# Softmax weights kept in PSUM, their sums split between GpSimd and the value matmul, and the first recurrence unit prepared inside the attention

## The chip, the cores and the metric

The kernel runs on one core of one Trainium2 chip. The metric is the device time of one execution in microseconds (us). The core has five engines that run their own instruction queues and meet through semaphores: TensorE (PE: matmul, with its weight loads as PEld), VectorE (DVE), ScalarE (ACT), GpSimd (POOL) and SyncE (SP, which issues DMAs here). Each engine works through its queue in order: an instruction that waits holds up everything behind it on that engine.

## The reference

One layer of a hybrid backbone runs on 1024 latent and 256 context tokens of width 1024. What matters here is the token mixer. Both branches read the same projected input `z = h @ w_in`:

```python
s = jnp.einsum('bqkgd,bskd->bkgqs', qi, kf) * scale
p = jax.nn.softmax(s, axis=-1)
return jnp.einsum('bkgqs,bskd->bqkgd', p, vf)
...
kv = jnp.einsum('bhnck,bhncv->bhnkv', k_end, v)
def step(s, inp):
    dec, kv_n = inp
    return dec[..., None] * s + kv_n, s
```

The attention has 8 query heads of 64 and 2 key heads; latent queries see 512 cached and 1024 latent keys, context queries the 256 context keys. The second branch is a gated linear recurrence with 4 heads, run forwards and backwards. Gates, an output projection and a squared-ReLU MLP follow.

## The kernel before

Every product of weights and activations that matters is made with values split into a high part (fp32r, the format that PE takes at full pace) and a low part, value minus high part; three matmuls stand for one. After a front part (normalisation, queries, keys and values, up to about 177 us) the attention runs, then the recurrence, then the projections and the MLP.

**The attention** (`attention`, class `Unit`) has 20 units: for each of the two key heads, eight units of 512 latent queries of one head against 12 blocks of 128 keys, and two units that hold 256 context queries of two heads against 2 blocks. A unit does this:

- `load_q`, `load_q2` load the queries (SP); `top` multiplies queries and keys (high parts) block by block and VectorE takes the maximum of each row; `top_row` transposes the four columns of maxima into rows, which four small DMAs put into row 64 of the second query operand, so that the score matmul subtracts the maximum by itself.
- `score(k)` for each key block: two matmuls (L725) into a bank of the PSUM ring `s`; ACT takes the exponential (L727) and a copy rounded to fp32r, the high part (L729); VectorE makes the low part (L730); POOL adds the exponentials into the accumulator `pacc` (L735, L737).
- `value`: two blocks at a time, each with two matmuls (L748) of the high and the low weights against V. V's 128 columns are V's 64 high columns and its 64 low ones, so rows 0 to 63 and 64 to 127 of the bank `ps_v` are added at the end (L752, L753).
- `sums`, `scale`: four fp32 matmuls of one column (L759) sum `pacc` over the keys, VectorE takes the reciprocal, PE transposes it, ACT copies it, POOL stores it to DRAM (`RR`), loads it back over 64 rows and multiplies (L773); SP stores the result.

**What sets the order.** PE's order is written out by hand. `attention` makes a list of events with a time in slots, one slot being one key block, sorts it and issues it. Between events a `Filler` hands out matmuls of the projections for the recurrence (L318 to L320 and L335 to L337, 277 us of them). Other engines' queues and SP's are ordered by a scheduler at build time. The recurrence (`hgrn`, class `HUnit`) has 24 units; `prep` loads a gate and a query block (`uf`, `uq`), makes two running products on VectorE (L891, L892) and several products on POOL and VectorE; `keys_t` transposes the keys on PE (L953). Before, the first `prep` stands in `hgrn`, after the attention and its filler have ended.

**Where the data lie.** SBUF tiles come from rings named by letters, with as many buffers as `RINGS` says; a new tile waits for the release of an old one. PSUM has eight banks of 128 rows by 512 fp32 columns, in the rings g, v, s and t.

Of the kernel before, what the change touches and what calls it, by code (L numbers as in the profile page):

```python
# [45 lines left out]
def build(ctx, tc, I, O, C):  # L46
# [25 lines left out]

    PSB = {"g": 2, "v": 1, "s": 3, "t": 2}
    ring_of_two, turn = [True], [0]

    def PS(tag, shape=(P, 512)):
        if tag == "g" and not ring_of_two:
            turn[0] += 1
            tag = "v" if turn[0] % 3 == 0 else tag
        return ps.tile(list(shape), F32, tag=tag, name="ps_" + tag, bufs=PSB[tag])  # L80

# [26 lines left out]
    def store(out, in_):  # L108
        g_.dma_start(out=f32(out), in_=f32(in_))  # L109

    def f32(ap):
        return ap.bitcast(F32)
# [486 lines left out]
    for idx in range(len(steps)):  # L599
# [23 lines left out]
        if kc == 0:  # L623
            if t > 0:
                front_prep(evs)
            banks = [PS(x) for x in ("sssv", "ggss", "sv")[t]]
        cols_next = t == 0 and kc % 2 == 1 and kc < KC - 1
# [43 lines left out]
    class Unit:  # L671
# [49 lines left out]
        def score(self, k):  # L721
            kg, b = self.kt[k]
            pq = PS("s")
            for var, q in enumerate((self.q1, self.q2)):
                pe.matmul(pq, K[self.g][var][kg][:, b * P:(b + 1) * P], q, start=(var == 0), stop=(var == 1))  # L725
            e = S(name="pexp")
            s_.activation(e, pq, AF.Exp)  # L727
            hi, lo = S(dt=F32R, name="pTh"), S(dt=F32R, name="pTl%d" % (k % 2))
            s_.activation(hi, e, AF.Copy)  # L729
            v.tensor_tensor(lo, e, f32(hi), op=ALU.subtract)  # L730
            if k == 0:
                self.acc = e
            elif k == 1:
                first, self.acc = self.acc, S(name="pacc")
                g_.tensor_tensor(self.acc, first, e, op=ALU.add)  # L735
            else:
                g_.tensor_tensor(self.acc, self.acc, e, op=ALU.add)  # L737
            self.pt[k] = hi, lo

        def value(self, p2):  # L740

            if p2 == 0:
                self.pv = PS("v")
            last = self.nb - 1
            for k in (2 * p2, 2 * p2 + 1):
                kg, b = self.kt[k]
                for j, x in enumerate(self.pt.pop(k)):
                    pe.matmul(self.pv, V[self.g][kg][:, b, :], x, start=(k == 0 and j == 0), stop=(k == last and j == 1))  # L748
            if k == last:
                tm, self.o = S((64, 512), name="pvt"), S((64, 512), name="oa")  # L750
                with tc.high_priority(offset=400):
                    s_.activation(tm, self.pv[64:128], AF.Copy)  # L752
                    v.tensor_tensor(self.o, self.pv[0:64], tm, op=ALU.add)  # L753

        def sums(self):

            pt = PS("t")
            for b in range(4):
                pe.matmul(pt[:, b:b + 1], self.acc[:, b * P:(b + 1) * P], one0[:, 0:1], start=True, stop=True)  # L759
            self.rs = T(4, "rs")  # L760
            v.reciprocal(self.rs, pt[:, 0:4])

        def scale(self):

            pt = PS("t")
            pe.transpose(pt[0:4, 0:P], self.rs, ident)
            r = S((4, P), name="prow")
            s_.activation(r, pt[0:4, 0:P], AF.Copy)
            row = RR[self.h][self.t]
            store(row.rearrange("o (b n) -> (o b) n", b=4), r)  # L770
            o, rb = self.o, S((64, 512), name="prb")
            g_.dma_start(out=rb, in_=row.broadcast_to([64, 512]))
            g_.tensor_tensor(o, o, rb, op=ALU.mult)  # L773
            oa = OA[self.h // 2][self.t]
            if self.t < 2:
                d0 = (self.h % 2) * 64
                dma(oa[d0:d0 + 64, :], o)
            else:
                dma(oa.rearrange("(h d) n -> d h n", h=2), self.view(o))

    RR = [[DR((1, 512), "RR%d_%d" % (h, t)) for t in range(3)] for h in range(8)]
    K = [[[None] * 4 for _ in range(2)] for _ in range(2)]
    V = [[None] * 4 for _ in range(2)]

    def load_k(g, kg, var):
# [8 lines left out]
    def load_v(g, kg):  # L794
        V[g][kg] = S((P, KG[kg] // P, P), F32R, name="Vl")
        dma(V[g][kg], VS[kg][:, :, g, :])

    def attention(fill):
        units = []
# [6 lines left out]
        for u in units:  # L806
            ev = []
            if u.t == 2:
                ev += [(-13.3, load_k, (u.g, 3, 0)), (-3.3, load_v, (u.g, 3))]
            elif u.g not in seen:  # L810
                seen.add(u.g)
                ev += [(a, load_k, (u.g, kg, 0)) for kg, a in enumerate((-13.4, -13.3, -13.2))]
# [12 lines left out]
        for a, f, x in events:  # L825
            fill.to((a - e0) / (e1 - e0))
            f(*x)
        ring_of_two.pop()

# [43 lines left out]
    class HUnit:  # L873
# [8 lines left out]
        def prep(self):  # L882
# [5 lines left out]

            c, e = S(name="ucp"), S(name="usf")
            if d == 0:  # L890
# [139 lines left out]
    def hgrn(fill):  # L1030

        units = [HUnit(h, d, t) for h in range(4) for d, t in ((0, 0), (0, 1), (1, 1), (1, 0), (0, 2), (1, 2))]
        fwd = {u.h: {} for u in units}
# [6 lines left out]
        tot, done, st = sum(share), 0.0, None  # L1040
        units[0].prep()
        units[0].keys_t()
# [60 lines left out]
    while pending:  # L1103
        fz.add(1.0)
        flush(1.0)
    attention(fz)
    fz.rest()
    R = S(name="R")
    g_.memset(R, 0.0)
    g_.memset(R.rearrange("p (c i) -> p c i", i=32)[:, :, 0:1], 1.0)  # L1110
    fg = Filler(with_ada([z_ch(GL + 256 * c, gl_consume(c)) for c in range(8)], 10), 194.0)
# [693 lines left out]
```

## Time and profile before

| | us |
|---|---|
| median of three runs | 2119.05 (2113.95 to 2119.84) |
| profiled execution | 2115.53 |
| its span | 2113.4 |
| PE busy | 2015.6 |
| VectorE, ScalarE, GpSimd busy | 1437.2, 958.2, 675.8 |

The profile lists busy time by engine, groups of instructions by source line, waits (who waited for whom, total, number, longest), and a timeline. A row names line, engine, operation, output<-inputs and size. PE's records overlap: one of 512 columns is shown with 0.39 us, while the next one starts 0.23 us after it. A wait is put down to the instruction whose signal came last.

### The profile page before, as it was taken

To read this page: it belongs to the slowest core of one execution; us is meant where nothing else is said; L and a number is where in the kernel's file an instruction comes from. 1 tells how busy PE (TensorE), PEld (TensorE's weight loads), DVE (VectorE), ACT (ScalarE), POOL (GpSimd) and SP (SyncE) were. 2 spreads that over 40 slices of the span, in tenths; PEclk is the share of its full clock that TensorE was granted. 3 is DMA by queue.
4 is the path that set the end of the run, shared out by engine and by line. 5 is a ranking of instruction groups with operands and counts; after the bars stand their busy time and mean duration, and the time that the engine had idled before them with its cause. 6 is when DMAs were issued, how large, how long until landed. Compare 5 with 4: busy or idle time off the path is not lost.

```text
span 2113.4 us, 31691 instructions
## 1 busy us (share of the span) xinstructions
PE 2015.6 (95%) x11436; PEld 1696.6 (80%) x11436; DVE 1437.2 (68%) x2385; ACT 958.2 (45%) x1802; POOL 675.8 (32%) x715
## 2 busy tenths in 40 slices
PE   6899999999999959999999999999999999999998
PEld 4687788877778848888888888998888888888886
DVE  4784777787787776797543734876666666567786
ACT  4763565555555512222330323765545444333442
POOL 1471455665454754554302200222122210000010
PEclk9999999999999979999999999999999999999999
DMA  9464222142221244554554532674444469545773
GB/s 293 129 189 145 89 91 91 51 145 71 80 78 58 78 135 123 177 173 152 159 172 140 185 111 109 215 224 161 148 160 147 168 223 372 181 147 178 219 261 127
DMA packets 236957, 325.21 MB, mean 154 GB/s; under 512 B 22024, under 2 KB 153264, under 8 KB 236800
## 3 DMA queue, kind: packets, MB, share of 16 engines
q1 hardware_dynamic: 222784, 280.87, 41.6%
q0 software_dynamic: 14016, 42.32, 5.7%
q8 instruction: 90, 1.47, 0.3%
q14 instruction: 67, 0.55, 0.1%
HBM read 235.46 MB, written 87.61 MB: 153 GB/s over the span
## 4 chain that ended last, share of the span: by engine, by line
PE 42%; issue 15%; POOL 4%; DVE 3%; DMA 2%; ACT 1%; SPq 0%; POOLq 0%; DVEq 0%; ACTq 0%
POOL AF L109 4%; PE ps_g L318 3%; PE ps_g L319 3%; PE ps_g L320 3%; PE ps_s L1606 2%; PE ps_s L1607 2%; PE ps_s L1608 2%; PE ps_v L318 1%; PE ps_g L1608 1%; PE ps_t L1606 1%; PE ps_g L1606 1%; PE ps_g L1607 1%; PE ps_t L1607 1%; PE ps_t L1608 1%; PE ps_v L320 1%
## 5 line engine op out<-in xcount | busy, mean ns | idle before, releaser
L737 POOL TENSOR_TENSOR pacc<-pacc,pexp 128x512 f32<-128x512 f32 x160 | 230.2, 1439 | 111.7 <-ACT pexp L727 68.6
L730 DVE TENSOR_TENSOR pTl<-pexp,pTh 128x512 fp32r<-128x512 f32 x200 | 229.8, 1152 | 48.7 <-ACT pTh L729 47.3
L318 PE MATMUL ps_g<-hs,wsp 128*128 128x512 f32 (+1 forms) x688 | 249.9, 363 | 0.0
L320 PE MATMUL ps_g<-hs,wsp 128*128 128x512 f32 (+1 forms) x688 | 241.6, 351 | 0.8 <-DVE wsp L290 0.8
L319 PE MATMUL ps_g<-hs,wsp 128*128 128x512 f32 (+1 forms) x688 | 241.8, 351 | 0.0
L289 ACT ACTIVATE wsp<-wraw 128x1024 fp32r<-128x1024 f32 x110 | 109.4, 996 | 267.9 <-PE ps_g L319 70.4
L290 DVE TENSOR_TENSOR wsp<-wraw,wsp 128x1024 fp32r<-128x1024 f32 x110 | 139.2, 1266 | 130.4 <-ACT wsp L289 130.1
L727 ACT ACTIVATE pexp<-ps_s 128x512 f32<-128x512 f32 x200 | 119.3, 597 | 163.9 <-PE ps_s L725 124.7
L708 DVE TENSOR_REDUCE mx<-ps_t 128x1 f32<-128x512 f32 (+1 forms) x208 | 136.8, 664 | 72.5 <-PE ps_t L707 71.7
L289 ACT ACTIVATE ah<-ar 128x640 fp32r<-128x640 f32 (+1 forms) x112 | 81.0, 724 | 189.3 <-PE ps_v L1607 102.3
L318 PEld LDWEIGHTS ps_g<-hs,wsp 128*128 128x128 f32 x688 | 131.4, 191 | 20.3 <-issue 2.9
L320 PEld LDWEIGHTS ps_g<-hs,wsp 128*128 128x128 f32 x688 | 131.0, 190 | 18.9 <-DVE wsp L290 1.0
L290 DVE TENSOR_TENSOR ah<-ar,ah 128x640 fp32r<-128x640 f32 (+1 forms) x112 | 89.8, 802 | 80.4 <-ACT ah L289 79.2
L319 PEld LDWEIGHTS ps_g<-hs,wsp 128*128 128x128 f32 x688 | 131.3, 191 | 16.5
L729 ACT ACTIVATE pTh<-pexp 128x512 fp32r<-128x512 f32 x200 | 126.0, 630 | 7.6
L171 POOL TENSOR_TENSOR frst<-ms,mexp 128x1 f32<-128x1 f32 x10 | 11.1, 1111 | 363.3 <-DVE ssf L1695 278.5
L335 PE MATMUL ps_g<-wsp,hs 128*128 128x256 f32 x400 | 115.8, 289 | 0.0
L337 PE MATMUL ps_g<-wsp,hs 128*128 128x256 f32 x400 | 112.8, 282 | 0.0
L336 PE MATMUL ps_g<-wsp,hs 128*128 128x256 f32 x400 | 112.7, 282 | 0.0
L707 PE MATMUL ps_t<-Kl,Ql 128*128 128x512 f32 x192 | 78.6, 410 | 12.5 <-DMA Ql<-QS 5.7
L725 PE MATMUL ps_s<-Q,Kl 128*128 128x512 f32 x200 | 79.0, 395 | 5.8 <-DMA Q<-mrow 3.0
L336 PEld LDWEIGHTS ps_g<-wsp,hs 128*128 128x128 f32 x400 | 75.9, 190 | 6.6
(490 smaller groups left out, 5827.3 us busy)
## 6 DMA issues: line engine op xcount, KB each, us to landing
ar<-AF SPq DMA_DIRECT2D x112, 320.0 KB, 3.3
wraw<-in_w_ff SPq DMA_DIRECT2D x32, 1024.0 KB, 5.9
wr<-in_w_ff SPq DMA_DIRECT2D x128, 256.0 KB, 4.3
wraw<-in_w_in SPq DMA_DIRECT2D x18, 1024.0 KB, 5.9
wraw<-in_w_ada SPq DMA_DIRECT2D x16, 1024.0 KB, 5.5
AF<-a POOLq DMA_DIRECT2D x48, 256.0 KB, 2.8
AF<-t POOLq DMA_DIRECT2D x48, 256.0 KB, 2.5
wa<-in_w_ada SPq DMA_DIRECT2D x32, 256.0 KB, 6.2
```

Source lines behind the costliest of these rows:

```text
L289: s_.activation(hi, raw, AF.Copy)
L290: v.tensor_tensor(lo, raw, f32(hi), op=ALU.subtract)
L318: pe.matmul(out, hi[:, k, :], mh, start=(first and k == 0), stop=False)
L319: pe.matmul(out, hi[:, k, :], ml, start=False, stop=False)
L320: pe.matmul(out, lo[:, k, :], mh, start=False, stop=(last and k == kcs - 1))
L335: pe.matmul(po[:, bb, :], mh[:, off:off + P], wh[:, k % 4, :], start=(k == 0), stop=False)
L336: pe.matmul(po[:, bb, :], mh[:, off:off + P], wl[:, k % 4, :], start=False, stop=False)
L708: v.tensor_reduce(self.mx[:, i:i + 1], pq[:, 0:n], axis=AX.X, op=ALU.max)
L727: s_.activation(e, pq, AF.Exp)
L729: s_.activation(hi, e, AF.Copy)
L730: v.tensor_tensor(lo, e, f32(hi), op=ALU.subtract)
L737: g_.tensor_tensor(self.acc, self.acc, e, op=ALU.add)
```

## The change

1. **Exponentials in PSUM.** ACT writes the exponential back into the score's bank; the high part is copied from there, and VectorE's subtraction reads the bank and the high part. A score bank is thus held until the low part is made. The ring `s` has two banks instead of three, and a new ring `w` has one.
2. **Sums in two parts.** POOL adds the high parts. The low parts go through a second value operand `V2`, V's 64 high columns beside 64 columns of ones, into the bank `ps_w`: rows 0 to 63 are low weights times V's high columns, rows 64 to 127 the sum of the low parts. (The product of low weights and V's low columns, which was made before, is left out.) One fp32 matmul with a selector (`sel1`: 64 columns of zeros, 64 of ones) adds the sum of `pacc` to rows 64 to 127. ACT copies one row, VectorE adds rows 0 to 63 to the output.
3. **The reciprocal goes through DRAM.** The row is stored (`SR`), loaded back as 128 x 4, inverted, stored (`RR`) and loaded over 64 rows: four DMAs on POOL's queue where there were two. The transpose and the four matmuls go.
4. **Order.** Loads, maxima and the row of maxima move ahead by up to 2.1 slots; a value step is now one block, issued 2.6 to 4.2 slots after its score. The query tiles move to the ring of 20 buffers, `pacc` to one of two, the low parts to one of three.
5. **First recurrence unit.** `R` and the first unit's `prep` become an event 3.8 slots before the last unit's end; `keys_t` of that unit stays at the start of `hgrn`.
6. Outside the attention every third tile of `s` comes from `w`, as one of `g` came from `v` before.

The core of the diff:

```diff
-            e = S(name="pexp")
-            s_.activation(e, pq, AF.Exp)
-            hi, lo = S(dt=F32R, name="pTh"), S(dt=F32R, name="pTl%d" % (k % 2))
-            s_.activation(hi, e, AF.Copy)
-            v.tensor_tensor(lo, e, f32(hi), op=ALU.subtract)
+            s_.activation(pq, pq, AF.Exp)
+            hi, lo = S(dt=F32R, name="pTh"), S(dt=F32R, name="pTl")
+            s_.activation(hi, pq, AF.Copy)
+            v.tensor_tensor(lo, pq, f32(hi), op=ALU.subtract)
+            if k == 1:
+                self.acc = S(name="pacc")
+            if k > 0:
+                g_.tensor_tensor(self.acc, f32(self.pt[0][0]) if k == 1 else self.acc, f32(hi), op=ALU.add)
...
+            pe.matmul(self.pv, V[self.g][kg][:, b, :], hi, start=(k == 0), stop=(k == last))
+            pe.matmul(self.pl, V2[self.g][kg][:, b, :], lo, start=(k == 0), stop=False, skip_group_check=True)
...
-            pt = PS("t")
-            for b in range(4):
-                pe.matmul(pt[:, b:b + 1], self.acc[:, b * P:(b + 1) * P], one0[:, 0:1], start=True, stop=True)
-            self.rs = T(4, "rs")
-            v.reciprocal(self.rs, pt[:, 0:4])
+            pe.matmul(self.pl, sel1[0], self.acc, start=False, stop=True, skip_group_check=True)
+            r = S(name="prow")
+            with tc.high_priority(offset=400):
+                s_.activation(r[64:65], self.pl[64:65], AF.Copy)
+                v.tensor_tensor(self.o, self.pl[0:64], self.o, op=ALU.add)
+            row, inv, rs = SR[self.h][self.t], RR[self.h][self.t], T(4, "rs")
+            store(row, r[64:65])
+            g_.dma_start(out=rs, in_=row.rearrange("o (p j) -> (o p) j", j=4))
+            v.reciprocal(rs, rs)
+            store(inv.rearrange("o (p j) -> (o p) j", j=4), rs)
...
-            ev += [(-12.9, u.load_q, ()), (-5.9, u.load_q2, ()), (-2.9, u.top_row, ())]
+            ev += [(-15.0, u.load_q, ()), (-6.9, u.load_q2, ()), (-3.4, u.top_row, ())]
-            ev += [(-11.6 + 8.2 * j / len(tops), u.top, x) for j, x in enumerate(tops)]
+            ev += [(-13.1 + 8.8 * j / len(tops), u.top, x) for j, x in enumerate(tops)]
-            ev += [(2 * p2 + 3.6, u.value, (p2,)) for p2 in range(u.nb // 2)]
-            ev += [(u.nb + 3.3, u.sums, ()), (u.nb + 4.3, u.scale, ())]
+            ev += [(k + 2.6 + max(0, 1.6 - 0.4 * k), u.value, (k,)) for k in range(u.nb)]
+            ev += [(max(u.nb + 2.2, u.nb - 1 + 4.3), u.sums, ()), (u.nb + 6, u.scale, ())]
...
+        events.append((s0 - 3.8, meanwhile, ()))
```

On PE, around a unit's sums (the sixth unit's), before: the sums write a bank of the ring t, and the next unit's first value matmuls follow four rows later. Names are those of the tiles: `ps_t`, `ps_v` banks, `pTh` and `pTl` the high and low weights.

```order
L759 MATMUL ps_t<-one_127,pacc 128x1 x4
L335 MATMUL ps_g<-wsp,hs 128x256
L336 MATMUL ps_g<-wsp,hs 128x256
L337 MATMUL ps_g<-wsp,hs 128x256
L748 MATMUL ps_v<-pTh,Vl 128x512
L748 MATMUL ps_v<-pTl_4262,Vl 128x512
L748 MATMUL ps_v<-pTh,Vl 128x512
L748 MATMUL ps_v<-pTl_4296,Vl 128x512
```

The same place now:

```order
L755 MATMUL ps_w<-pacc,sel_2303 128x512
L708 MATMUL ps_t<-Kl,Qp 128x256
L336 MATMUL ps_g<-wsp,hs 128x256
L337 MATMUL ps_g<-wsp,hs 128x256
L338 MATMUL ps_g<-wsp,hs 128x256
...
L708 MATMUL ps_t<-Kl,Ql 128x512
L726 MATMUL ps_s<-Ql,Kl 128x512
L726 MATMUL ps_s<-Q_4054,Kl 128x512
...
L745 MATMUL ps_v<-pTh,Vl 128x512
L746 MATMUL ps_w<-pTl,V_2504 128x512
```

The sums and the next unit's first low value matmul now write the same bank, `ps_w`, with filler, maxima and a score between them.

On POOL, at the last unit's end, before (`pacc` is that unit's accumulator, `ze` a gate product, `RR3_1` its reciprocal's row):

```order
L737 TENSOR_TENSOR pacc_8054<-pacc_8054,pexp_8237 128x512
L737 TENSOR_TENSOR pacc_8054<-pacc_8054,pexp_8265 128x512
L737 TENSOR_TENSOR pacc_8054<-pacc_8054,pexp_8288 128x512
L737 TENSOR_TENSOR pacc_8054<-pacc_8054,pexp_8310 128x512
L868 TENSOR_TENSOR ze_8339<-ze_8339,hnb_110 128x512
L109 DMA RR3_1_1951<-prow_8401 4x128
```

The same place now (`uf`, `usf`, `uw` are the first recurrence unit's tiles):

```order
L913 TENSOR_SCALAR uf_8055<-uf_8055 128x512
L941 TENSOR_TENSOR usf_8060<-uf_8055,usf_8060 128x512
L937 TENSOR_TENSOR uw_8080<-uq_8056,um_8065 128x512
L937 TENSOR_TENSOR uw_8082<-uq_8056,um_8065 128x512
L881 TENSOR_TENSOR ze_8121<-ze_8121,hnb_110 128x512
L937 TENSOR_TENSOR uf_8055<-usf_8060,um_8065 128x512
L735 TENSOR_TENSOR pacc_7873<-pacc_7873,pTh_8105 128x512
...
L735 TENSOR_TENSOR pacc_7873<-pacc_7873,pTh_8134 128x512
L735 TENSOR_TENSOR pacc_7873<-pacc_7873,pTh_8154 128x512
L881 TENSOR_TENSOR ze_8205<-ze_8205,hnb_110 128x512
L110 DMA SR3_1_1951<-prow_8224 16x1x32
```

Five operations of the first recurrence unit stand ahead of the last three additions, which the sums' matmul on PE needs.

On SP, the loads of the second recurrence unit (`uf`, `uq` from `FD0_0_1`, `QD0_1`), before and now:

```order
L106 DMA GD1_2_2012<-ze_8417 128x512
L106 DMA OA1_1_1921<-oa_8359 64x512
L106 DMA uv_8467<-VD0_0_2001 128x4x128
L106 DMA uf_8480<-FD0_0_1_1978 128x512
L106 DMA uq_8481<-QD0_1_1966 128x512
```

```order
L107 DMA GD1_2_2036<-ze_8272 128x512
L107 DMA uf_8297<-FD0_0_1_2002 128x512
L107 DMA uq_8298<-QD0_1_1990 128x512
L107 DMA GT0_0_2037<-ze_8394 128x512
L107 DMA OA1_1_1921<-oa_8196 64x512
```

The load stands behind the last gate store in both; it is now ahead of the last attention output's store instead of behind it.

More of the change, by code (lines that the diff above doesn't have):

```diff
@@ L70, in build @@
     sl = pool("sl")
-    PSB = {"g": 2, "v": 1, "s": 3, "t": 2}
-    ring_of_two, turn = [True], [0]
+    PSB = {"g": 2, "v": 1, "s": 2, "w": 1, "t": 2}
+    third, rings_of_two = {"g": "v", "s": "w"}, [True]
+    turn = {"g": 0, "s": 0}
     def PS(tag, shape=(P, 512)):
-        if tag == "g" and not ring_of_two:
-            turn[0] += 1
-            tag = "v" if turn[0] % 3 == 0 else tag
+        if tag in turn and not rings_of_two:
+            turn[tag] += 1
+            tag = third[tag] if turn[tag] % 3 == 0 else tag
         return ps.tile(list(shape), F32, tag=tag, name="ps_" + tag, bufs=PSB[tag])
@@ L625, in build @@
                 front_prep(evs)
-            banks = [PS(x) for x in ("sssv", "ggss", "sv")[t]]
+            banks = [PS(x) for x in ("sswv", "ggss", "wv")[t]]
         cols_next = t == 0 and kc % 2 == 1 and kc < KC - 1
@@ L725, in score, with value @@
                 pe.matmul(pq, K[self.g][var][kg][:, b * P:(b + 1) * P], q, start=(var == 0), stop=(var == 1))
-            e = S(name="pexp")
-            s_.activation(e, pq, AF.Exp)
-            hi, lo = S(dt=F32R, name="pTh"), S(dt=F32R, name="pTl%d" % (k % 2))
-            s_.activation(hi, e, AF.Copy)
-            v.tensor_tensor(lo, e, f32(hi), op=ALU.subtract)
-            if k == 0:
[L732 to L743, printed above, removed]
+            s_.activation(pq, pq, AF.Exp)
[6 more added lines that the diff above has]
+                g_.tensor_tensor(self.acc, f32(self.pt[0][0]) if k == 1 else self.acc, f32(hi), op=ALU.add)
+            self.pt[k] = hi, lo
+        def value(self, k):
+            if k == 0:
+                self.pv, self.pl = PS("v"), PS("w")
             last = self.nb - 1
[L745 to L748, printed above, removed]
+            kg, b = self.kt[k]
+            hi, lo = self.pt.pop(k)
+            pe.matmul(self.pv, V[self.g][kg][:, b, :], hi, start=(k == 0), stop=(k == last))
+            pe.matmul(self.pl, V2[self.g][kg][:, b, :], lo, start=(k == 0), stop=False, skip_group_check=True)
             if k == last:
@@ L783, in build @@
     V = [[None] * 4 for _ in range(2)]
+    V2 = [[None] * 4 for _ in range(2)]
+    sel1 = []
     def load_k(g, kg, var):
@@ L887, in prep @@
             dma(q[:, 0:n], QD[h][t])
-            c, e = S(name="ucp"), S(name="usf")
+            c, e, R = S(name="ucp"), S(name="usf"), Rs[0]
             if d == 0:
@@ L1030, in hgrn @@
     def hgrn(fill):
-        units = [HUnit(h, d, t) for h in range(4) for d, t in ((0, 0), (0, 1), (1, 1), (1, 0), (0, 2), (1, 2))]
+        units = hunits
         fwd = {u.h: {} for u in units}
@@ L1040, in hgrn @@
         tot, done, st = sum(share), 0.0, None
-        units[0].prep()
         units[0].keys_t()
```

37 lines of the change are left out of this document (23 added, 14 removed), and 4 rows, old and new, of the table RING_OF.

## The prediction

> **What bounds the kernel now.** I read the page's first part, then the busy time by windows, then the waits of PE inside the stretch that the change touches, then the timeline around its end.
>
> ```profile
> span 2113.4 us, 31691 instructions
> PE 2015.6 (95%) x11436; PEld 1696.6 (80%) x11436; DVE 1437.2 (68%) x2385; ACT 958.2 (45%) x1802; POOL 675.8 (32%) x715
> ...
> 177.00:745.00 568.00, 537.26 (x3088) 451.23 (x3087) 422.89 (x580) 318.60 (x575) 314.45 (x246) 0.99 0.27 84
> 745.00:773.00 28.00, 3.79 (x32) 2.85 (x31) 18.13 (x28) 3.37 (x6) 12.87 (x15) 0.60 0.52 169
> ```
>
> The columns of the two window rows are length, then busy time of PE, PEld, DVE, ACT and POOL, then granted clock. TensorE bounds the kernel. In the attention, from 177 to 745, it is idle 568 - 537.3 = 30.7 us of 200 key steps (2.84 us a step, called a slot below). Behind it, from 745 to 773, it is idle 24.2 us. Only these 55 us, and PE's own work, can become less.
>
> ```profile
> PE ps_t L707 <- DMA Qp<-QS: 6.1, 4, 2.8
> PE ps_t L707 <- DMA Ql<-QS: 5.7, 4, 3.5
> PE ps_t L707 <- DVE mx L708: 5.0, 8, 1.6
> PE ps_t L715 <- DVE ngm L710: 4.2, 6, 1.2
> PE ps_s L725 <- DMA Q<-mrow: 3.0, 4, 1.3
> PE ps_s L725 <- DMA Ql<-QS: 2.8, 1, 2.8
> ...
> 742.36 0.95 PE L759 MATMUL ps_t<-one,pacc 128*128 128x1 f32 x8
> 743.17 0.36 PE L335 MATMUL ps_g<-wsp,hs 128*128 128x256 f32 x1
> ...
> 745.95 1.07 PE L186 MATMUL ps_g<-wraw,ada_l 128*32 128x256 f32 x16
> 771.23 1.09 PE L953 MATMUL ps_t<-ident,usf 128*128 128x128 f32 x4 [24.21 <-DVE usf L924]
> ...
> 784.69 0.60 PE L953 MATMUL ps_t<-ident,usf 128*128 128x128 f32 x4
> ```
>
> The waits (total, times, longest) fall into 17.6 us for queries and maxima that come late by DMA, and 9.2 us for VectorE's maxima. The 24 us are the transposes of the first recurrence unit's keys waiting for a preparation that starts after the attention.
>
> **Attention: VectorE.** The 200 subtractions now read one operand from PSUM.
>
> ```profile
> L730 DVE TENSOR_TENSOR pTl<-pexp,pTh x200: 658/1150/4115, 200.1 to 736.6; 128x512 fp32r<-128x512 f32 x100
> L753 DVE TENSOR_TENSOR oa<-ps_v,pvt 64x512 f32<-64x512 f32 x20 | 13.5, 676 | 1.9 <-ACT pvt L752 1.4 <-issue 0.5
> L737 POOL TENSOR_TENSOR pacc<-pacc,pexp 128x512 f32<-128x512 f32 x160 | 230.2, 1439 | 111.7 <-ACT pexp L727 68.6 <-ACT prow L768 30.0 <-ACT mrow L717 9.0
> ```
>
> Today, with both operands in SBUF, one takes between 0.66 and 4.1 us, median 1.15. The same operation with one operand in PSUM, L753, averages 0.676 beside the same busy POOL. So VectorE loses about 200 x (1.150 - 0.676) = 95 us of its 423; the bounds are that gain and nothing. It is worth only what PE waits for VectorE's maxima, 9.2 us: I take 6 off.
>
> [...] The rows show 0.676 against an undisturbed 0.658.
>
> **Attention: loads and maxima ahead.** The query load leads its first maximum by 1.9 slots instead of 1.3 (1.7 us more), the row of maxima its first score by 3.4 instead of 2.9 (1.4 us more), and the query's ring grows from 2 to 20 buffers. Taking 1.7 us off each wait leaves 1.8 of Ql, 1.1 of Qp and 1.1 of the late score: 13.6 us go. But the loads stay in SP's queue behind output stores that now wait for two more DMA trips. I take 11 off (bounds 5 and 17.6).
>
> **Attention: the sums on PE.** Eight records and one transpose go, one fp32 matmul of 512 columns comes.
>
> ```profile
> 238.38 0.40 PE L748 MATMUL ps_v<-pTl,Vl 128*128 128x512 f32 x1
> 238.61 0.40 PE L748 MATMUL ps_v<-pTh,Vl 128*128 128x512 f32 x1
> ...
> L335 PE MATMUL ps_g<-wsp,hs 128*128 128x256 f32 x318 | 91.6, 288 | 0.0
> L748 PE MATMUL ps_v<-pTl,Vl 128*128 128x512 f32 x200 | 79.3, 397 | 1.5 <-DVE pTl L730 1.5
> L186 PE MATMUL ps_g<-wraw,ada_l 128*32 128x256 f32 x128 | 8.6, 385 | 0.0
> L766 PE MATMUL ps_t<-ident,rs 128*4 128x128 f32 x20 | 5.4, 271 | 0.0
> ```
>
> Removed are 743.17 - 742.36 = 0.81 us and some 0.2 of the transpose's 0.27. An fp32 matmul leaves two records (80 calls, 160 records at L759). From 256 to 512 fp32r columns a record grows by 109 ns, so its fixed part is 179; a full fp32 record of 256 columns takes 385, so 206 is columns, and 512 columns 0.41. Two make 0.82. Bounds are 0.46 (the 0.23 pace of fp32r, twice) and 1.18 (two whole records of 0.59). At 0.8: 0.2 x 20 = 4 us off (bounds 11 off and 4 on). The value matmuls keep their number and width.
>
> **Attention: the low parts' bank.** This is the new wait. One bank, ps_w, collects the low parts; it is free for the next unit only when the sums' matmul has run, ACT has copied a row, and then VectorE has added.
>
> ```profile
> L727 ACT ACTIVATE pexp<-ps_s 128x512 f32<-128x512 f32 x200 | 119.3, 597 | 163.9 <-PE ps_s L725 124.7 <-POOL pacc L737 16.9 <-issue 13.3
> L729 ACT ACTIVATE pTh<-pexp 128x512 fp32r<-128x512 f32 x200 | 126.0, 630 | 7.6
> ```
>
> A row copy costs its 512 columns, so 0.6 like L727; with 0.68 for the add and about 0.3 for the matmul's tail and signals (the 0.40 record against its 0.23 pace, plus a hop) that is 1.6 us. Between the sums and the next unit's first write PE has, in the order shown, six to nine filler matmuls, a score pair and one or two maxima, about 2.1 us. Alone it hides. ACT and VectorE take it in turn behind an exponential pair (1.2) or a maximum (0.68), so sometimes it doesn't; meanwhile VectorE's maxima queue behind the add. I put 0.4 us on each of 20 units: 8 us (bounds 0 and 40, the upper being 2 us each, when one such piece stands ahead on both engines).
>
> Costed at nothing: two score banks instead of three, each held for 0.60 + 0.63 + 0.68 plus hops, about 2.2 us, against two slots, 5.7; the cover is gone once either engine holds a bank 3 us longer. A ring of three for the low parts: the value of step k leaves 2.6 slots after its score, sooner than step k+3 needs it (first steps of a unit are within 0.3 slot). Two more DMA trips on POOL, 1.1 us of issue and about 4 of waiting per unit, during which the next unit's additions queue:
>
> ```profile
> 356.96 1.47 POOL L737 TENSOR_TENSOR pacc<-pacc,pexp 128x512 f32<-128x512 f32 x1 [0.23 <-ACT pexp L727]
> ...
> 366.84 0.95 PE L759 MATMUL ps_t<-one,pacc 128*128 128x1 f32 x8
> ```
>
> a unit's last addition ends 8 us before its sums. Eight loads and fills of the ones: ACT is idle 250 us of this stretch.
>
> Attention: -11 - 6 - 4 + 8 = -13 us.
>
> **The end.** The first unit's preparation moves in front of the last unit's three last additions on POOL.
>
> ```profile
> 735.85 6.18 POOL L737 TENSOR_TENSOR pacc<-pacc,pexp 128x512 f32<-128x512 f32 x4
> ...
> 747.87 1.09 SPq L106 DMA_DIRECT2D uf<-FD  x1
> ...
> 756.72 1.22 DVE L891 TENSOR_TENSOR_SCAN ucp<-R,uf 128x512 f32<-128x512 f32 x1 [9.28 <-DMA uf<-FD]
> 759.22 1.45 POOL L900 TENSOR_SCALAR uf<-uf 128x512 f32<-128x512 f32 x1 [9.20 <-DVE usf L893]
> 761.88 1.25 POOL L928 TENSOR_TENSOR usf<-uf,usf 128x512 f32<-128x512 f32 x1
> 764.00 2.05 POOL L924 TENSOR_TENSOR uw<-uq,um 128x512 f32<-128x512 f32 x2 [0.88 <-DVE um L915]
> 766.01 1.57 POOL L924 TENSOR_TENSOR uf<-usf,um 128x512 f32<-128x512 f32 x1
> 770.11 0.97 DVE L924 TENSOR_TENSOR usf<-usf,um 128x512 f32<-128x512 f32 x1
> ...
> L109 POOL DMA_DIRECT2D RR<-prow x19 | 10.6, 555 | 0.0
> ...
> DMA to landing us min/median/max: 1.5/1.6/3.7
> ```
>
> Before, the last sums (742.4) start as POOL's last addition ends (742.0). POOL now does 1.45 + 1.25 + 2.05 + 1.57 = 6.3 us more there and about 2.7 for one issue and trip, less 11 x 0.14 for additions undisturbed by VectorE: the sums come at about 750, so PE waits some 7 us that it did not. Behind them stand 0.8 of their own, 36 filler matmuls of 256 columns at half of the 0.23 pace, 4.2, and L186, 1.1, so the first keys are transposed at about 756 instead of 771, unhindered. The second unit's keys follow 784.69 - 771.23 = 13.5 us of PE later, at 770. Are they ready? Their load stands in SP's queue behind the last gate store, which waits for POOL's product, which stands behind the reciprocal's store: 750 + 0.8 + 0.6 + (0.55 + 1.6) twice + 0.2 + 0.55 + 1.3 + 0.5 = 758. Landing takes up to 8.8 (747.87 to 756.7, beside weight loads); from scan to keys took 756.72 to 771.1 = 14.4, of which 11 to 14 stays, since the third unit's scans again stand in it. So 777 to 781, say 778: 7 us before today's 784.7. The gap doesn't close, it splits: 7 us at the sums, 8 at the second keys. The end is worth -7; the bounds are -24 (neither is late) and 0.
>
> ```profile
> 772.97 0.63 PE L320 MATMUL ps_g<-hs,wsp 128*128 128x512 f32 x1
> ...
> 774.59 0.39 PE L318 MATMUL ps_g<-hs,wsp 128*128 128x512 f32 x1
> ```
>
> The granted clock was 0.60 there, and matmuls after the idle stretch took 0.63 us instead of 0.39. [...]
>
> Sum: 2115.5 (the profiled execution) - 13 - 7 = 2095.5. That execution lies 3.5 us under the median of the three runs, so for a median I say 2119 - 20 = **2099 us**.
>
> **Rivals.** (a) Both stretches nearly close: all 17.6 + 9.2 us of waits go, 4 of work, the low bank hides, and the end gives 14: 45 off, 2074. For it: VectorE sheds a fifth of its work. Against: the SP queue. (b) Nothing nets: the loads stay late behind SP (5 off), the sums and the low bank cost 1, the end gives 0: 2115, within 0.3% (6.4 us, about what a measurement here can tell from no change). POOL 7 us later still at the last sums does this to the end; a PSUM operand that doesn't free VectorE would take the 6 from the rest. (c) Slower: the low bank's handover. At 2.4 us a unit instead of 0.4 it costs 40 more than I assumed, and gives 2139; it decides from 1.7 us a unit on. For it speaks that three engines pass the bank in order; against, PE's 2.1 us of other work.
>
> **How the numbers follow.** Forecast 0.62, (a) 0.14, (b) 0.13, (c) 0.11. Around the forecast, the unknown sizes (loads 5 to 17.6, bank 0 to 16, end 0 to 15) give about 2085 to 2112. The range goes down to (a) and up past (b), 2074 to 2120; (c) and the outer half of (a) are left out. Faster is the forecast and (a), less a little for its upper edge: 0.75; same 0.14; slower 0.11.
>
> **What would show it.** Right: L731 near 0.68 us with little spread; waits on Ql, Qp and mrow under 6 us; short waits of PE on ps_w at the first value of a unit; PE waiting for POOL at the last sums and for VectorE at the second L966. Wrong: no wait at those two places, or waits of PE on ps_w of over 1.7 us a unit, or on ps_s at the scores, which I costed at nothing.

## The result, and the profile after

The changed kernel is slower: 2147.89 us (median of 4 runs, 2144.16 to 2153.92) against 2116.5 of the kernel before beside it, a ratio of 1.0151 (95% interval 1.012 to 1.0182). The profiled execution took 2148.34 us, 32.8 more than that of before.

The page's first part and the windows that answer to those of before (length, then busy time of PE, PEld, DVE, ACT, POOL, then the granted clock; the last two columns, DMA, are not used). The attention now ends at 783, not 745:

```profile
span 2146.6 us, 31802 instructions
PE 2025.3 (94%) x11296; PEld 1697.0 (79%) x11296; DVE 1358.9 (63%) x2405; ACT 967.0 (45%) x1812; POOL 670.4 (31%) x757
...
177.00:783.00 606.00, 544.68 (x2942) 449.34 (x2941) 351.45 (x613) 325.95 (x583) 317.46 (x294) 0.97 0.27 81
783.00:811.00 28.00, 14.38 (x113) 11.06 (x111) 18.93 (x33) 4.08 (x8) 12.34 (x13) 0.82 0.58 188
```

In the attention PE is idle 606 - 544.7 = 61.3 us, where it was 30.7, and it is busy 7.4 us more. VectorE does 71 us less, and PE does not gain by it. Behind the attention the 28 us hold 14.4 us of PE's work where they held 3.8.

PE's waits from 177 to 800 (total, times, longest), and its row at the second recurrence keys:

```profile
PE ps_t L708 <- DMA Ql<-QS: 38.2, 13, 5.6
PE ps_t L708 <- DVE mx L709: 8.5, 11, 1.3
PE ps_t L708 <- DMA Qp<-QS: 7.6, 4, 3.7
PE ps_s L726 <- DVE pTl L731: 6.8, 2, 6.1
...
784.04 1.07 PE L187 MATMUL ps_g<-wraw,ada_l 128*32 128x256 f32 x16
812.16 1.12 PE L966 MATMUL ps_t<-ident,usf 128*128 128x128 f32 x4 [14.78 <-DVE usf L937]
```

The loss has one large entry: the first maximum of a unit waits for the unit's query (`Ql`) 38.2 us in 13 units; together with `Qp` that makes 45.8, where before it was 8.5 (5.7 at maxima, 2.8 at a score) + 6.1 = 14.6.

By place: the attention's last matmul of the adaptation weights (L186, now L187) moves from 745.95 to 784.04, +38.1. From there to the second keys it was 784.69 - 745.95 = 38.7 and is 28.1, -10.6. From the second keys to the end it was 1328.7 and is 1334.4, +5.7. The sum is +33.2 of span.

### The profile page after: what moved, and what is told of

It reads as the page before. It is cut to its first block, busy times and chain, and to the rows that moved or that the text cites. A ratio compares the mean times of both kernels' runs of the same rounds, so it can differ in the third digit from the quotient of the medians.

```text
span 2146.6 us, 31802 instructions
## 1 busy us (share of the span) xinstructions
PE 2025.3 (94%) x11296; PEld 1697.0 (79%) x11296; DVE 1358.9 (63%) x2405; ACT 967.0 (45%) x1812; POOL 670.4 (31%) x757
## 4 chain that ended last, share of the span: by engine, by line
PE 56%; DVE 4%; DMA 2%; ACT 1%; issue 1%; POOL 0%; SPq 0%; DVEq 0%; POOLq 0%; ACTq 0%
PE ps_g L319 3%; PE ps_g L321 3%; PE ps_g L320 3%; PE ps_v L319 2%; PE ps_g L1627 1%; PE ps_v L321 1%; PE ps_v L320 1%; PE ps_g L1625 1%; PE ps_g L1626 1%; PE ps_t L1625 1%; PE ps_t L1626 1%; PE ps_t L1627 1%; PE ps_s L1475 1%; PE ps_t L1473 1%; PE ps_t L1474 1%; PE ps_t L1475 1%
## 5 line engine op out<-in xcount | busy, mean ns | idle before, releaser
L735 POOL TENSOR_TENSOR pacc<-pacc,pTh 128x512 f32<-128x512 f32 x160 | 208.4, 1303 | 117.8 <-ACT pTh L730 102.8
L731 DVE TENSOR_TENSOR pTl<-ps_s,pTh 128x512 fp32r<-128x512 f32 x200 | 137.3, 687 | 114.0 <-ACT pTh L730 97.4
L728 ACT ACTIVATE ps_s<-ps_s 128x512 f32<-128x512 f32 x200 | 116.6, 583 | 198.5 <-PE ps_s L726 180.2
L320 PEld LDWEIGHTS ps_g<-hs,wsp 128*128 128x128 f32 x688 | 132.0, 192 | 17.6 <-issue 0.2
L708 PE MATMUL ps_t<-Kl,Ql 128*128 128x512 f32 x192 | 85.0, 443 | 46.7 <-DMA Ql<-QS 38.2
L730 ACT ACTIVATE pTh<-ps_s 128x512 fp32r<-128x512 f32 x200 | 119.4, 598 | 13.5 <-ACT ps_s L728 0.4
L172 POOL TENSOR_TENSOR frst<-ms,mexp 128x1 f32<-128x1 f32 x10 | 11.4, 1152 | 362.7 <-DVE ssf L1714 278.4
L336 PE MATMUL ps_g<-wsp,hs 128*128 128x256 f32 x400 | 117.6, 294 | 0.0
L338 PE MATMUL ps_g<-wsp,hs 128*128 128x256 f32 x400 | 114.5, 286 | 0.0
L337 PE MATMUL ps_g<-wsp,hs 128*128 128x256 f32 x400 | 114.4, 286 | 0.0
L708 PEld LDWEIGHTS ps_t<-Kl,Ql 128*128 128x128 f32 x192 | 37.1, 193 | 63.2 <-DMA Ql<-QS 42.5
```

The source lines that it names most:

```text
L320: pe.matmul(out, hi[:, k, :], ml, start=False, stop=False)
L336: pe.matmul(po[:, bb, :], mh[:, off:off + P], wh[:, k % 4, :], start=(k == 0), stop=False)
L708: pe.matmul(pq[:, 0:n], self.q1[:, b * P:(b + 1) * P], K[self.g][0][self.kts[i]], start=True, stop=True)
L728: s_.activation(pq, pq, AF.Exp)
L730: s_.activation(hi, pq, AF.Copy)
L731: v.tensor_tensor(lo, pq, f32(hi), op=ALU.subtract)
```

## The experiments

**Two theories.** SP issues its DMAs in order (in the second view below a store that waits holds what stands behind it until 291.61). One place of the attention shows how the load of the next unit's query stands there. SP's rows from 289 on before the change (start, length; `Q<-mrow` are the four row DMAs of the unit that is about to begin), and PE's first maximum:

```profile
289.46 0.64 SPq L106 DMA_DIRECT2D OA<-oa  x1
290.58 2.45 SPq L106 DMA_DIRECT2D Q<-mrow  x4
293.46 0.34 SPq L106 DMA_DIRECT2D FD<-ze  x1
293.89 0.38 SPq L106 DMA_DIRECT2D Ql<-QS  x1
...
297.33 0.50 PE L707 MATMUL ps_t<-Kl,Ql 128*128 128x512 f32 x1 [0.30 <-DMA Ql<-QS]
```

The same place in the changed kernel:

```profile
284.21 8.04 SPq L107 DMA_DIRECT2D OA<-oa  x2
292.34 2.45 SPq L107 DMA_DIRECT2D Q<-mrow  x4
294.89 0.53 SPq L107 DMA_DIRECT2D FD<-ze  x1
295.52 0.38 SPq L107 DMA_DIRECT2D Ql<-QS  x1
...
299.27 0.80 PE L708 MATMUL ps_t<-Kl,Ql 128*128 128x512 f32 x1 [5.12 <-DMA Ql<-QS]
```

In both the query load is issued behind the rows of the previous unit, and these need that unit's last maximum. The first row of the second view joins two output stores, issued at 284.21 and 291.61; between them SP waits for POOL's product, which ends at 291.58. So here the rows wait for the store: ACT had their values ready at 289.77. It is so at one more place, near 590 us (there with a weight load and another store between); elsewhere the first row is issued within 0.8 us of ACT's copy. Elsewhere the maximum decides, and with it the times in the list: in the next unit's count the rows stood at -2.9 - 12 = -14.9 and stand at -15.4; the first maximum stood at -11.6 and stands at -13.1. From rows to first maximum there were 3.3 slots and are 2.3. *Theory 1*: the load's own place in the list (-12.9, now -15.0) was moved, but not past the rows, so the maximum alone came forward. *Theory 2* (the rival): the reciprocal's two more trips make the output store `OA` late, it holds SP, and all behind it. The place above speaks for it: its wait of 5.12 us and the one near 590, 5.59 us, are the two longest of the 13.

In the experiments' numbers, "Ql" is the sum of PE's waits on `Ql`, at the maxima and at the scores.

**Old times** (changed kernel, offsets of before).

```diff
-(a, load_k, (u.g, kg, 0)) for kg, a in enumerate((-15.5, -15.4, -15.3))
+(a, load_k, (u.g, kg, 0)) for kg, a in enumerate((-13.4, -13.3, -13.2))
-(-15.0, u.load_q, ()), (-6.9, u.load_q2, ()), (-3.4, u.top_row, ())
+(-12.9, u.load_q, ()), (-5.9, u.load_q2, ()), (-2.9, u.top_row, ())
-(-13.1 + 8.8 * j / len(tops), u.top, x)
+(-11.6 + 8.2 * j / len(tops), u.top, x)
```

> The changed kernel, with the times of its loads, maxima and rows of maxima put back to those of the kernel before. Theory 1 (the query load stands in SP's queue behind the previous unit's four row DMAs, and the change left 2.3 slots instead of 3.3 between that row and the first maximum): PE's waits for Ql fall from 38 us to 5 to 12, with 4 us of slow restarts, so about 2113 to 2120 us. Theory 2 (the four DMA trips of the reciprocal delay the output stores, which hold SP): the waits stay above 30 us and the time within 5 us of 2148.

Measured: 2134.45 us, ratio 1.0071 (1.0052 to 1.0091); Ql 26.9. The times bring 13 us back, not 31: under half of what theory 1 had promised. The rest was open.

**Query early** (changed kernel, query and keys' loads ahead of the rows, maxima as changed).

```diff
-(a, load_k, (u.g, kg, 0)) for kg, a in enumerate((-15.5, -15.4, -15.3))
+(a, load_k, (u.g, kg, 0)) for kg, a in enumerate((-18.0, -17.9, -17.8))
-(-15.0, u.load_q, ()), (-6.9, u.load_q2, ()), (-3.4, u.top_row, ())
+(-17.4, u.load_q, ()), (-6.9, u.load_q2, ()), (-3.4, u.top_row, ())
```

> The changed kernel, with the query loads (and the first key loads) 2.4 slots earlier still, so that they stand ahead of the previous unit's row DMAs in SP's queue. Theory 1: PE's waits for Ql fall below 5 us, the rest unchanged, about 2108 to 2116 us. Theory 2: the loads now stand ahead of the output store too, so the waits fall as well; this run does not tell the two apart, the others do. Were a third cause at work (the transfers themselves are slow), the waits would stay above 20 us.

Measured: 2111.51 us, ratio 0.996 (0.9939 to 0.998). PE's waits:

```profile
PE ps_t L966 <- DVE usf L937: 14.9, 1, 14.9
PE ps_t L708 <- DVE mx L709: 12.3, 14, 3.2
PE ps_s L726 <- DVE pTl L731: 10.9, 6, 6.1
PE ps_s L726 <- DMA Q<-mrow: 8.3, 4, 3.3
```

No wait for a query is left, and 36 us of the changed kernel's time are gone with it. PE is also busy 536.65 us from 177 to 745.8, with the same instructions for which the changed kernel took 544.68. Matmuls at a lower clock explain the 8 us: in the changed kernel's attention the granted clock is 0.50 in eight stretches of 3.4 or 6.8 us, 41 us in all, one at each of the eight waits of 3.0 us or more; here it is 0.50 in five, 20.5 us. PE was busy for 32.9 and 17.6 us of them; half of that, an estimate of what the lower clock cost, is 16.5 and 8.8.

**Output stores on POOL's queue** (changed kernel) and **preparation back behind the attention** (changed kernel).

```diff
-                dma(oa[d0:d0 + 64, :], o)
+                store(oa[d0:d0 + 64, :], o)
...
-        events.append((s0 - 3.8, meanwhile, ()))
...
     attention(fz, first_unit)
     fz.rest()
+    first_unit()
```

> The changed kernel, with the attention's output stores issued from POOL's queue instead of SP's. Theory 1: SP still issues four row DMAs ahead of each query load, the waits for Ql fall only by what the output stores added, to 25 to 35 us, 2138 to 2148 us. Theory 2: the waits fall below 10 us, 2112 to 2120 us.

> The changed kernel, with the preparation of the first recurrence unit back behind the attention. If moving it brought what the traces say (from the attention's last matmul to the second keys 27.2 us instead of 37.7, less the 6.1 us that PE waits for a score bank while VectorE prepares), this is 3 to 6 us slower than the changed kernel, 2151 to 2154 us. If the preparation's place costs more than it brings, it is faster, below 2146.

Measured: 2146.26 us (1.0146, 1.0102 to 1.019) with Ql 24.7, and 2153.28 us (1.0169, 1.0141 to 1.0196) with Ql 34.6 and 26.4 us at the first keys. Theory 2 alone falls: without the stores on SP the time does not move in the timed runs (2140.83 to 2159.51). But it has a part: the profiled execution, the shortest of the four, waits 13 us less, and the two longest waits fall from 5.12 and 5.59 us to 2.51 and 3.23. The preparation inside the attention looks worth about 5 us here, but the intervals of the two kernels overlap.

**Old times and stores on POOL together.**

> The changed kernel with the old times of loads, maxima and rows, and with the attention's output stores on POOL's queue. Theory 1 (the query load is late because SP must first issue what stands ahead of it, which the new times and the later output stores both lengthened): the two repairs add up, PE's waits on Ql fall from 23.7 us (old times alone) to under 8, as before the change, and the time to 2113 to 2122 us. Rival, that the stores only move their wait to POOL, whose additions then come late: Ql falls, but PE waits on ps_w or POOL in its place, and the time stays at 2130 to 2140.

Measured: 2133.66 us (1.006, 1.0039 to 1.0081), Ql 22.7. Theory 1 as written here falls too: the two repairs don't add up. Something else keeps the queries late when all times are those of before.

**The kernel before with new times**, **with early loads**, and **with nothing but the ring**. All three have the query tiles in the ring of 20 buffers, as the changed kernel has. The edits, the ring first, then the new times (with those of keys and maxima as in the change), then the early loads:

```diff
-"Ql": "F"
+"Ql": "X"
...
-(-12.9, u.load_q, ()), (-5.9, u.load_q2, ()), (-2.9, u.top_row, ())
+(-15.0, u.load_q, ()), (-6.9, u.load_q2, ()), (-3.4, u.top_row, ())
...
-(-12.9, u.load_q, ()), (-5.9, u.load_q2, ()), (-2.9, u.top_row, ())
+(-17.4, u.load_q, ()), (-5.9, u.load_q2, ()), (-2.9, u.top_row, ())
```

> The kernel before, with only the changed kernel's times of loads, maxima and rows (and its ring for the query). Theory 1 in its strong form (the new order on SP's queue suffices): waits on Ql rise from 8.5 us to over 20, the time to 2128 to 2140. Theory 2 (it takes the longer trip of the reciprocal, with the output store that waits for it on SP): Ql stays under 12 and the time is 2108 to 2121; the forecast's own step, taken alone, would be 2108.

> The kernel before, with nothing changed but the early query and key loads of the fastest variant so far (17.4 slots ahead, query tiles in the ring of 20). If the early load alone makes that variant fast, the kernel before gains what it waited for Ql (8.5 us) and some of Qp: 2106 to 2112 us, level with the variant's 2111.5, and the rest of the change nets nothing. If the PSUM operand, the sums and the end are worth what the traces suggest (some 10 us at the end alone), the kernel before gains at most its 8.5 us and stays above the variant, at 2110 to 2119.

> The kernel before with only the query tiles in the ring of 20, all times unchanged: a control for the kernel before with the new times, which needed that ring. If the times made it slow, this one stays at 2112 to 2122 us with 5 to 12 us of waits on Ql. If the ring did (a query tile waits for the release of an older tile of a busy ring), waits on Ql rise above 20 and the time to 2130 to 2165.

Measured: new times 2162.91 us (1.0203, 1.0178 to 1.0227), early loads 2117.88 (0.9989, 0.9975 to 1.0003), the ring alone 2133.43 (1.0077, 1.0054 to 1.01). PE's waits for queries, and other long ones, in the three, in this order:

```profile
PE ps_t L707 <- DMA Ql<-QS: 35.9, 11, 6.6
PE ps_v L748 <- ACT pTh L729: 9.8, 1, 9.8
```

```profile
PE ps_t L707 <- DVE mx L708: 8.3, 11, 1.7
PE ps_t L715 <- DVE ngm L710: 7.3, 4, 2.6
```

```profile
PE ps_t L707 <- DMA Ql<-QS: 17.2, 8, 6.0
PE ps_t L707 <- DMA Qp<-QS: 3.8, 1, 3.8
```

So times and ring, without PSUM, sums, reciprocal or preparation, make the kernel before 44 us slower, more than the 9 to 21 us that theory 1 had given: theory 2 is not needed. (9.8 us are another wait on SP's order: a weight load is issued late, at 732.46, and ACT, which works in order, waits 11.4 us for it ahead of the exponentials.) And the ring alone, which I had thought harmless, costs 17 us. It is not the ring's buffers that are late, since with the same ring and early loads no query waits. It is the place on SP. In the order of the two traces, 11 of the 16 query loads now have a DMA ahead of them that stood behind them. At four, where a context unit lies between, it is the second of two sets of rows; these four wait 0.5 us in all. The long waits, 6.0 and 5.6 us, are at two loads that now stand right behind weight loads (`wraw`); one of the two waited 3.5 us before too. The other, near 360 us, before:

```order
L106 DMA Ql<-QS_1_139 128x512
L106 DMA Qp<-QS_2_140 128x512
L106 DMA wraw<-in_w_ada 128x8x256
```

And with the ring alone changed:

```order
L106 DMA Qp<-QS_2_140 128x512
L106 DMA wraw<-in_w_ada 128x8x256
L106 DMA VD_2_2003<-ze 128x512
L106 DMA wraw<-in_w_in 128x8x256
L106 DMA Ql<-QS_1_139 128x512
```

The load has fallen behind two weight loads and a store; PE's longest wait for a query in that kernel, 6.0 us, follows there.

**Only the loads keep their new times** (changed kernel; maxima, rows and second loads at the times of before).

```diff
-(-6.9, u.load_q2, ()), (-3.4, u.top_row, ())
+(-5.9, u.load_q2, ()), (-2.9, u.top_row, ())
-(-13.1 + 8.8 * j / len(tops), u.top, x)
+(-11.6 + 8.2 * j / len(tops), u.top, x)
```

> The changed kernel with its own times of the loads, but maxima, rows and second query loads at the times of before. The query load (15.0 slots ahead) is then listed 0.1 slot ahead of the previous unit's row DMAs (14.9) instead of 0.4 behind them, and the first maximum follows 3.4 slots later instead of 1.9. Theory 1: waits on Ql, 38.2 us, fall under 10, and the time to 2110 to 2122. If a load's place against the rows is not the point, Ql keeps 20 us or more, as with all old times, and the time is 2128 to 2140.

Measured: 2109.99 us, ratio 0.9964 (0.9947 to 0.998), no wait on `Ql`. SP's rows at the same unit, and the first maximum, which no longer waits:

```profile
289.54 0.64 SPq L107 DMA_DIRECT2D OA<-oa  x1
290.27 0.53 SPq L107 DMA_DIRECT2D Ql<-QS  x1
...
291.38 2.46 SPq L107 DMA_DIRECT2D Q<-mrow  x4
...
295.89 0.39 PE L708 MATMUL ps_t<-Kl,Ql 128*128 128x512 f32 x1
```

The output store stands ahead of the load here as well; it is issued at 289.54, as before the change (289.46), 2 us sooner than in the changed kernel. That the maxima are later again does not explain the gain alone: "Old times" has the same maxima and rows, differs in nothing but the offsets of query and key loads, and waits 26.9 us. There the load at this place is issued behind the rows, at 294.30 instead of 290.27, and PE waits 1.29 us. Theory 1 holds in a corrected form: what counts is what stands ahead of the load on SP (rows, at some places a late store, and weight loads), not by how many slots it was listed ahead.

**Old times and the old ring** (changed kernel, `Ql` in ring F, `pacc` in X).

> The changed kernel with the old times of loads, maxima and rows, and with its query tiles back in the ring of two buffers (the accumulator back in the ring of 20). On SP the query load then stands in places ahead of a second unit's row DMAs again, as before the change. If the ring is the rest of the loss, waits on Ql fall from 26.9 us to under 14, and the time from 2134 to 2108 to 2120, with the end's gain left over. If the rest comes from the longer reciprocal or the score banks, the time stays at 2128 to 2138.

Measured: 2123.24 us, ratio 1.0012 (1.0001 to 1.0024), Ql 11.3. The two tiles' rings were 11 of the 15 us that were left; the band given ended 3 us lower. Its waits, among others:

```profile
PE ps_s L726 <- DVE pTl L731: 12.1, 6, 7.0
PE ps_t L708 <- DMA Ql<-QS: 9.1, 5, 4.5
```

**A better version.** From the early-load variant on: the preparation of the first two recurrence units cut into steps, one every slot or so.

```diff
-        events.append((s0 - 3.8, meanwhile, ()))
+        events += [(s0 - 15.0 + i, meanwhile, (0,)) for i in range(13)]
+        events += [(s0 - 11.5 + 0.85 * i, meanwhile, (1,)) for i in range(13)]
...
+        next(steps[i], None)
```

`prep` has become a generator here, which yields after each larger operation; `next` runs it to its next yield.

> The early-load variant, with the preparation of the first two recurrence units cut in steps that stand one by one in the last 15 slots of the attention. Theory: the 6.1 us wait for a score bank behind the preparation and the 14.9 us wait for the second unit's keys both go: 2111.5 - 6 - 14 = 2091, or up to 2100 where the third unit's keys now wait for theirs. Rival, that the steps delay low parts and maxima inside the attention by as much, or that the gap moves wholly to the third unit: 2108 to 2115.

Measured: 2103.92 us (0.992, 0.9898 to 0.9942), 4 us over the band's upper end: the second keys no longer wait, and no single wait for a score bank is over 2.6 us. But the attention ends 6.7 us later (753.50 against 746.82). It was then tried with the maxima back at -11.6 (and rows at -3.2), with the stores on POOL, and with both:

> The variant with early loads and the preparation in steps, its maxima back at the times of before (from 11.6 slots ahead), the rows at 3.2 instead of 3.4. With the loads early, the maxima no longer need their lead: if the maxima's waits for VectorE (11.9 us) and the scores' waits for rows (6.8) come from the denser start, some 5 to 10 us go: 2094 to 2099 us. Rival, that rows now come late because the maxima end 0.9 slots later: waits on rows rise above 10 us, 2106 to 2115.

> The same variant with the attention's output stores on POOL's queue. Theory 2, now for the rows alone: the row DMAs come late (6.8 us of waits at the scores) because the output store, which waits for the longer trip of the reciprocal, stands ahead of them on SP. If so the waits on rows fall under 2 us and the time to 2096 to 2100. If the rows are late by their own chain (transpose, copy, four small DMAs), they stay at 5 to 8 us and the time at 2101 to 2108.

> The variant with early loads, preparation in steps and the maxima at the times of before, with the output stores on POOL's queue as well. If the two gains add up (the maxima's times 11 us, the stores 7): 2083 to 2090 us, with waits on rows under 5 us. If both work on the same wait: 2090 to 2097.

Measured: 2092.82 us (0.9887, 0.9866 to 0.9907), 2096.85 (0.9904, 0.9882 to 0.9925) and 2092.31 (0.987, 0.9853 to 0.9887). The maxima's later start takes their waits from 11.9 to 1.7 us, while the rows' rise from 6.8 to 9.4; the stores on POOL take the rows' from 6.8 to 4.1. Together they bring no more than the first alone, as far as the runs can tell. This is 23 to 27 us under the kernel before. The two longest groups of waits of the last one:

```profile
PE ps_s L726 <- DVE pTl L731: 16.9, 9, 3.2
PE ps_s L726 <- DMA Q<-mrow: 3.3, 3, 1.4
```

What is left is mostly the score bank, which is held until the low part is made.

## Why the prediction was wrong, point by point

**The step that failed: "Attention: loads and maxima ahead", taken at -11 us.** It took 1.7 us off each wait because "the query load leads its first maximum by 1.9 slots instead of 1.3". Both places were read from the list, but the load is not issued at its place in the list. It is issued when SP is through with what stands ahead, the previous unit's rows, and those moved by only 0.5 slot while the maximum moved by 1.5. In place of 11 us off, the waits on Ql and Qp rose from 14.6 to 45.8, and PE ran slowly after them for some 8 more (544.68 against 536.65 busy). The step's own warning, that the loads "stay in SP's queue behind output stores", named the queue and only one of the neighbours, and gave it no price: the bounds of 5 and 17.6 held no loss. With the loads alone moved ahead 36 us of the changed kernel's time are gone ("Query early"), more than the 31 that were lost. SP's rows show how what stands ahead holds a load: between the stores issued at 284.21 and 291.61 it issues nothing, and the query load, which needs nothing that is late, follows 0.1 us behind what stands ahead of it. The step also took the query's larger ring as harmless; by itself it costs the kernel before 17 us by changing the order on SP.

**VectorE, -6 us.** The durations came as forecast:

```profile
L731 DVE TENSOR_TENSOR pTl<-ps_s,pTh x200: 660/691/694, 198.8 to 771.6; 128x512 fp32r<-128x512 f32 x100
```

The median fell from 1150 to 691 ns, and VectorE does 71 us less in the attention (forecast 95; the first preparation now lies in it too). In the changed kernel PE gains nothing by it: 8.5 us of waits for maxima, where it was 9.2. The maxima's new times hide the gain. With early loads PE waits 12.3 us on `mx` when the maxima start early; with the loads' new times alone, and the maxima at their old ones, it waits 0.6 on `mx` and 2.3 + 1.4 on `ngm`; the kernel before with early loads waits 8.3 and 7.3. Three waits of the variant with the loads alone:

```profile
PE ps_s L726 <- DVE pTl L731: 10.5, 5, 7.1
PE ps_s L726 <- DMA Q<-mrow: 8.6, 5, 3.3
...
PE ps_t L708 <- DVE mx L709: 0.6, 1, 0.6
```

What PE no longer waits for maxima, it waits for a score bank and for rows: this variant's attention ends at 744.58, that of the kernel before with early loads at 746.53. The two differ in the rest of the change too, so VectorE's share of this is argued, not shown. At their shortest, 660 ns with one operand in PSUM stands against 658 with both in SBUF; the longest fell from 4115 ns to 694, so the long tail is gone.

**The sums on PE, -4 us.** About 3 us. The fp32 sums take 20.4 us for 20 pairs of records, 1.02 a pair, where 0.8 was taken between bounds of 0.46 and 1.18:

```profile
L755 PE MATMUL ps_w<-pacc,sel 128*128 128x512 f32 x40 | 20.4, 592 | 0.0
```

But records overlap, so I count starts: from the first record of the sums to the second matmul behind them, less the 0.23 or 0.12 us of the one between, it was 0.89 us and is 0.86; the transpose took 0.11 by the same count. That is 0.14 x 20 = 2.8 us. PE's busy time doesn't tell it. It is 541.15 us (177 to 745.5) in the kernel before with early loads and 536.65 (177 to 745.8) in the changed one with them, -4.5, but 537.26 in the kernel before itself; stretches at the lower clock move it by as much.

**The low parts' bank, +8 us, and rival (c).** It doesn't happen: in the changed kernel PE's waits show none on `ps_w`, and in the variants the low value matmuls wait for it at most 3.1 us in all. The time came out on the rival's side, by another mechanism.

**Score banks, costed at nothing.** That was wrong: PE waits 6.8 us for a low part in the changed kernel, 10.9 in "Query early" and 10.5 in "Only the loads", where queries come in time. The cover was to be gone "once either engine holds a bank 3 us longer", and the preparation, which I had moved past POOL's additions only, does that on VectorE: its scans and products stand there from 759.09 to 768.40, ahead of a low part, and PE waits once for 6.06 us.

```profile
769.13 0.79 PE L726 MATMUL ps_s<-Ql,Kl 128*128 128x512 f32 x1 [6.06 <-DVE pTl L731]
```

**The end, -7 us.** From the attention's last matmul to the second keys it is -10.6; with the 6.06 us for the score bank, which the same move costs inside the attention, it is -4.5. So it came near the forecast by luck, as the parts differ: PE doesn't wait for POOL at the last sums (forecast 7 us), and the second keys wait 14.8 (forecast 8). The gap did split, into a score bank and the second keys. Of the +5.7 behind, 3.4 lie at the program's very end: the last output lands 1.7 us after the end of its issue in both, but from the end of POOL's last operation to the end of the span it is 8.6 us (2138.02 to 2146.6) where it was 5.15 (2108.25 to 2113.4). Why is not shown; the other 2.3 were not traced.

## What to carry to other kernels

Where one queue issues all loads in order, the lead of a load is counted from the last instruction ahead of it on that queue that waits for something, or that moves much, not from its own place in a list: look in the order for what it has been moved past (one load was issued at 295.52 behind the rows, and at 290.27 ahead of them where the loads alone had moved). A load that is moved "earlier" and stays behind the same waiting DMA has not moved, and bringing its reader forward makes a wait. An engine that is relieved by 71 us gives at most what others waited for it (9.2 us here), and only where the order leaves them that gain. Operations put into a stretch with few buffers should be laid one by one, not in a block: that, and the maxima's old start, took the early-load variant from 2111.51 to 2092.82 us.

## What the runs showed of the hardware

Moving a tile between rings, without touching a time, changed the order of DMAs on SP and cost 17 us (2133.43 against 2116.18). In the changed kernel a query load took 3.2 to 4.0 us from issue to landing at most places (median 3.4), but 6.6 us (issued at 367.12) and 8.2 (at 517.87) where a weight load had been issued 0.5 us ahead of it.

After a wait PE was slow, but not always at once. Two first maxima of the changed kernel:

```profile
409.30 0.80 PE L708 MATMUL ps_t<-Kl,Ql 128*128 128x512 f32 x1 [3.00 <-DMA Ql<-QS]
409.89 0.63 PE L726 MATMUL ps_s<-Qp,Kl 128*128 128x512 f32 x1
...
448.65 0.50 PE L708 MATMUL ps_t<-Kl,Ql 128*128 128x512 f32 x1 [4.45 <-DMA Ql<-QS]
448.99 0.40 PE L726 MATMUL ps_s<-Ql,Kl 128*128 128x512 f32 x1
449.22 0.56 PE L726 MATMUL ps_s<-Q,Kl 128*128 128x512 f32 x1
449.58 0.63 PE L319 MATMUL ps_g<-hs,wsp 128*128 128x512 f32 x1
```

After 3.00 us idle the first matmul is slow (0.80, then 0.63 instead of 0.39); after 4.45 us the first two run at almost full pace and the slow ones begin 0.6 to 0.9 us later. The granted clock was 0.50 from 408.30 to 415.10 and from 449.30 to 452.70. In the early-load variant it fell behind a wait of 2.00 us:

```profile
429.30:432.70 3.40, 3.40 (x9) 2.67 (x10) 2.42 (x4) 1.18 (x2) 0.00 (x0) 0.51 0.02 5
```

The eight stretches of lower clock in the changed kernel's attention are 3.4 or 6.8 us long. The fall came behind a wait of 2.00 us, within one of 3.00 and, after one of 4.45, only some way into the work, so the length of one wait alone doesn't tell. Over the changed kernel's attention the lower clock made some 16 us of PE's busy time by the estimate above, 8 more than in the early-load variant, beside 61 us of idle time.
